# One tuned hybrid backbone: weights' low parts on VectorE, merge products queued behind the large ones, more large products in the merges

## The chip, the cores and the metric

The kernel runs on one core of one Trainium2 chip. The metric is device time in microseconds (us) of one launch; less is better. The median before is 4449.08 us over 3 runs (4446.22 to 4451.25). Engines: PE is TensorE, DVE is VectorE, ACT is ScalarE, POOL is GpSimd, SP issues DMAs.

## The reference

Two layers over 768 tokens (256 of context, 512 latent), width 1024, all in float32. Each layer projects its normalized input once and feeds three branches, of which the first is what matters here:

```
zl = hl @ w_in                       # 10112 columns: RWKV, convolution, attention, gates
def step(S, inp):                    # RWKV-7, both directions, 16 heads of 64
    r_t, w_t, k_t, v_t, kk_t, a_t = inp
    s_kk = einsum('bhij,bhj->bhi', S, kk_t)
    S = S * w_t - s_kk * (kk_t * a_t) + v_t * k_t
    return S, einsum('bhij,bhj->bhi', S, r_t)
out = sum_n(gate_n * (branch_n @ w_branch_n)) @ w_out
x   = x + mod * rms_norm(out);  x = x + mod * rms_norm(relu(h @ w1)**2 @ w2)
```

The second layer needs its output for the latent tokens only.

## The kernel before

**Large products.** Every matrix product with a weight is taken as three products of rounded parts: high times high, high of the weight times low of the operand, low of the weight times high of the operand (lines 409 to 414). `weight_half` (line 367) loads half a weight block (512 rows by 128 columns), ACT rounds it to its high part `wh` (line 328), and the remainder `wl = raw - wh` is taken by POOL when `lo_pool` is set (line 330) and else by DVE (line 332). There are three buffers each of `wh` and `wl`, and a half serves four steps of the contraction. `fill(n)` issues n such steps from a list of waiting jobs: six matmuls of 384 columns each over all 768 tokens, or three of 512 columns over the latent ones. Twenty-four matmuls use a half of the first kind, twelve one of the second.

**Recurrence.** The scan is cut in 12 chunks of 64 tokens and worked in eight rounds per layer, a pair of heads in each (`rwkv_phase`, from line 1127). A round turns on one serial path. `rw_front` makes the chunks' Gram matrices on PE (lines 809, 818) and DVE masks them (813). `rw_solve` inverts 32 by 32 triangular blocks on DVE: two transposes (854, 855), 30 pairs of a multiply (860) and an add (861) that depend on each other one by one, and two transposes back (862, 863). `rw_merge` joins the blocks for the two directions: 24 products of 32 by 32 each (891), copies by ACT (895), products again (904), copies and masks (900, 906). Then come `rw_batch` (920, 931), the chain over the chunks (`rw_chain`, 952 to 970) and, beside it, the next pair's keys and Grams, the convolution's 31 taps on DVE (470, 473) and the shift mixing of new inputs on DVE (657).

**What sets the order.** `weave` runs the parts as generators; each yields a time in us, and `pe` issues as many large products as that time by a ratio from `SCHED` calls for. While DVE solves, `fill(F['solve'] - 8)` has PE do large products (lines 1194 and 1235): 24 steps in layer 0, 32 in layer 1. The framework then schedules the recorded instructions by a cost model of its own and sets the order on each engine; an engine runs its queue in that order. Only what `keep_in_program_order` or `add_manual_dep` names is held in place: ACT's copies of line 895 stand behind the last high part of a weight. `pin` is never true, so the line that it guards does nothing.

`lo_pool` is False for the first inputs of a layer and its first solve, becomes True before the eight rounds (line 1195) and stays so through the phase that merges the branches; the MLP sets it to False.

Of the kernel before, what the change touches and what calls it, by code (L numbers as in the profile page):

```python
# [12 lines left out]
AF = mybir.ActivationFunctionType  # L13
# [6 lines left out]
KT = 8  # L20
# [24 lines left out]

SCHED = [dict(open=1.3, first=0.55, mid=0.5, end=0.4, solve=32, early=4, tap0=1, tap1=1, merge=0, sums=0, grams=0, rest=9, ln=9, pad=1, last=1.15, tap2=1),
         dict(open=1.2, first=0.4, mid=0.4, end=0.4, solve=40, early=5, tap0=0.8, tap1=0.8, merge=0, sums=0, grams=0, rest=9, ln=9, pad=1, last=0.85, tap2=1.1)]


def shape_constants():
# [24 lines left out]
class Kern:  # L77
# [319 lines left out]
    def fill(s, n=1):  # L397
        nc = s.nc
        for _ in range(min(n, len(s.jobs))):
            k, mh, ml, T, done, pre = s.jobs.pop(0)  # L400
            if k % 4 == 0:
                while s.halves and len(s.ready) < s.nw:
                    s.ready.append(s.weight_half(*s.halves.pop(0)))
                s.cur = s.ready.pop(0)
            if k == 0:
                s.jps = s.mm()
                s.jctx = (pre(),) if pre else ()
            wh, wl = s.cur
            for w, m, f in ((wh, mh, 0), (wh, ml, 1), (wl, mh, 2)):
                a = m(k)  # L410
                for b, t0, t1 in s.pieces(T):
                    ins = nc.tensor.matmul(s.jps[:, b, :t1 - t0], lhsT=w[:, k % 4, :], rhs=a[:, t0:t1], start=k == 0 and f == 0, stop=k == KT - 1 and f == 2)  # L412
                    if s.pin and f == 0 and b == 0:
                        s.tc.keep_in_program_order(ins)
            if k == KT - 1:
                done(s.jps, *s.jctx)

# [461 lines left out]
        nc.scalar.activation(out=bv[:, o:], in_=bv[:, o:], func=AF.Identity, bias=P['v']('rw_ln_b')[:, p:p + 1])  # L879
        nc.sync.dma_start(s.bv_d[p % 2][:, o:], bv[:, o:])  # L880

    def rw_merge(s, Q, d):

        nc, hi = s.nc, s.last_hi
        GL = s.big['GL', d]
        Dn, Dt = (s.Z[:, i:i + 384].rearrange("p (u t) -> p u t", t=32) for i in (1152 * d, 768 - 384 * d))
        one, two, c = (HI, LO, 0) if d else (LO, HI, 32)
        xp = s.g([128, 12, 32])
        for q in range(12):
            for h in range(2):  # L890
                nc.tensor.matmul(xp[two[h], q, :], lhsT=GL[one[h], h, q, c:c + 32], rhs=Dn[one[h], q, :], start=True, stop=True)
        TT = Q['TT', d] = GL.rearrange("p h c t -> p (h c t)")[:, 0:768].rearrange("p (c t) -> p c t", t=64)
        Xn = Dn
        for h in range(2):
            ins = nc.scalar.activation(out=Xn[two[h]], in_=xp[two[h]], func=AF.Copy, scale=-1.0)

            s.tc.add_manual_dep(ins.ins, hi.ins.name, mybir.DependencyInfo(mybir.DependencyClass.NoSync, mybir.DependencyReason.DATA), reason="weights first")
        yield 1.1 + s.sched['merge']
        for o, m in ((0, s.tlo), (32, s.thi)):
            nc.vector.tensor_scalar(out=TT[:, :, o:o + 32], in0=Dt, scalar1=m, scalar2=None, op0=ALU.mult)  # L900
        tr = s.g([128, 12, 32])
        for q in range(12):
            for h in range(2):
                nc.tensor.matmul(tr[one[h], q, :], lhsT=Xn[two[h], q, :], rhs=Dt[two[h], q, :], start=True, stop=True)
        for h in range(2):
            nc.scalar.activation(out=TT[one[h], :, c:c + 32], in_=tr[one[h]], func=AF.Copy, scale=-0.5)
        yield 1.1 + s.sched['merge']
# [171 lines left out]
    def run(s):  # L1079
        nc, tc, i = s.nc, s.tc, s.i  # L1080
        s.nraw, s.nw, s.lo_pool, s.turn = 2, 3, False, 0
        s.halves, s.ready, s.jobs = [], [], []
        s.cops, s.pin = [], False
        s.psum('gen')
        s.constants()
        s.xT_d = s.dp.tile([D, TOK], F32, name="xT_d")
        s.bv_d = [s.dp.tile([128, TOK], F32, name=f"bv_d{i}") for i in range(2)]
        s.oat = s.dp.tile([D, TOK], F32, name="oat")
        s.orw = s.dp.tile([D, TOK], F32, name="orw")
        s.ocv = s.dp.tile([D, TOK], F32, name="ocv")  # L1090
        s.spills = ([(C_Q + 128 * j, False, False) for j in range(8)] + [(C_AK + 128 * j, True, False) for j in range(4)] +
                    [(C_GATE + 128 * j, False, True) for j in range(24)])
        s.z = s.dp.tile([128 * len(s.spills), TOK], F32, name="z")
        s.kp = lambda d: d.rearrange("(k p) t -> p k t", p=128)
        PP = [s.load_params(0)]
        s.h_open()
        with ExitStack() as xc:
            X = xc.enter_context(tc.tile_pool(name="x0", bufs=1)).tile([128, KT, TOK], F32, name="X")
            sp = xc.enter_context(tc.tile_pool(name="n0", bufs=1))
            s.load_x(sp, X)  # L1100
            ss = s.ps2()
            for k in range(KT):
                s.ss_add(sp, ss, X[:, k], k, TOK)
            R = s.rstd(sp, ss, TOK, 1.0 / D, 0, CTX)
            for f in s.mod_steps(0, PP[0], sp, 0, 5):
                f()
            s.mod_pre(PP[0])
# [19 lines left out]
    def rwkv_phase(s, l, P, T):  # L1127
# [3 lines left out]
        with ExitStack() as rc:  # L1131
# [50 lines left out]
            s.rw_inputs(l, P, 0, T, I, 'krv')  # L1182
            s.fill(24)
            Q = s.rw_open(l, 0)
            s.pin = False
            spills(F['early'])
            s.weave(F['open'], prep(0, I, Q, lambda n: ()))
            s.conv_jobs(l, P, 0, T, s.ocv)
# [2 lines left out]
            s.rw_solve()  # L1191
            s.weave(3.0, rest(I))
            s.rw_inputs(l, P, 1, T, In, 'kr')
            s.fill(F['solve'] - 8)
            s.lo_pool = True
            old = None
            for p in range(8):
                ev = set()
# [14 lines left out]
                else:  # L1213
                    spills(len(todo))
                s.tratio = F['tap0'] if more else 1.2
                held = [s.rw_readout(l, P, p - 1, old, T, s.orw), note('ro')] if old else [note('ro')]
                gs = [chain(s.rw_merge(Q, 0), s.rw_batch(Q, 0, lat), note('b0'), wait('b1'), s.rw_chain(Q, lat, ev.add, wait('ro'))),
                      chain(s.rw_merge(Q, 1), s.rw_batch(Q, 1, lat), note('b1'))]
                if more:
                    gs.append(chain(prep(p + 1, In, Qn, wait, *held), wait('s3'), grams(In, Qn, 0), wait('s7'), grams(In, Qn, 1), wait('s11'), grams(In, Qn, 2)))  # L1220
                else:
# [4 lines left out]
                if more:  # L1226
# [5 lines left out]
                    s.weave(3.0, rest(I))  # L1232
                    if p < 6:
                        s.rw_inputs(l, P, p + 2, T, In, 'kr')
                    s.fill(F['solve'] - 8)
            s.taps(len(s.cops))
            s.pin = False

    def merge_phase(s, l, PP, T, acc):

# [208 lines left out]
```

## Time and profile before

| | |
|---|---|
| median of 3 runs | 4449.08 us |
| profiled execution, its own time | 4455.6 us |
| its span, first to last instruction | 4453.8 us |
| busy share of the span: PE, PEld, DVE, ACT, POOL | 94%, 77%, 60%, 41%, 19% |
| mean granted clock of TensorE | 0.956 of 2.4 GHz |
| recurrence of layer 0, of layer 1 | 150 to 1240 us, 2550 to 3580 us |

The span is 1.8 us shorter than the execution's own time. Windows are stretches of the span: for each engine busy us and, in brackets, the instructions begun, in the order PE, PEld, DVE, ACT, POOL; PEclk is the share of TensorE's full clock that was granted, as a mean over the stretch. The granted clock has two levels, 1.2 and 2.4 GHz.

### The profile page before, as it was taken

How to read it: one execution, taken by the hardware profiler on the slowest of the kernel's cores; microseconds unless marked ns; L12 is line 12 of the kernel's file. 1: busy time of each engine (PE TensorE's matmuls, PEld its weight loads, DVE VectorE, ACT ScalarE, POOL GpSimd, SP SyncE). 2: the span in 40 equal slices, each digit the busy share in tenths (PEclk: the TensorE clock that was granted, in tenths of full speed). 3: DMA queues.
4: the chain of work that ended last, by engine and by line, in shares of the span. 5: the costliest groups of instructions: out<-in, count | busy, mean ns of one | idle time of the engine just before them, and what ended most of it. 6: DMA issues, size and time to landing. Idle time of an engine off the chain costs nothing. (4 is left out here: it accounts for less than half of the span.)

```text
span 4453.8 us, 76934 instructions
## 1 busy us (share of the span) xinstructions
PE 4190.7 (94%) x31232; PEld 3412.5 (77%) x31232; DVE 2674.6 (60%) x4828; ACT 1817.7 (41%) x3562; POOL 837.4 (19%) x735
## 2 busy tenths in 40 slices
PE   6999999999998989899999899999999988898998
PEld 4888887888886678689999677877777775475886
DVE  3788778878945453232233568778778854443344
ACT  3454445444434442332222344545444534434332
POOL 0022121212112145300000102122122212262001
PEclk8999999999999999899999889999999979998999
DMA  4211211111134235343322221121111233142332
GB/s 166 66 46 52 60 59 55 57 50 57 60 96 163 68 97 166 119 149 129 103 79 64 66 60 56 48 61 49 54 54 59 65 104 101 57 140 63 96 95 81
DMA packets 438345, 364.05 MB, mean 82 GB/s; under 512 B 19022, under 2 KB 386792, under 8 KB 431848
## 3 DMA queue, kind: packets, MB, share of 16 engines
q1 hardware_dynamic: 417256, 279.43, 20.8%
q10 hardware_dynamic: 20736, 79.70, 4.9%
q8 instruction: 247, 4.05, 0.4%
q14 instruction: 106, 0.87, 0.1%
HBM read 299.29 MB, written 53.48 MB: 79 GB/s over the span
## 5 line engine op out<-in xcount | busy, mean ns | idle before, releaser
L328 ACT ACTIVATE wh<-raw 128x512 fp32r<-128x512 f32 x700 | 441.9, 631 | 1332.1 <-PE mm L389 561.2
L330 POOL TENSOR_TENSOR wl<-raw,wh 128x512 fp32r<-128x512 f32 x386 | 534.2, 1384 | 2008.5 <-ACT wh L328 1697.7
L412 PE MATMUL mm<-hh,wh 128*128 128x384 f32 (+1 forms) x2072 | 668.1, 381 | 11.6 <-ACT hh L347 4.0
L412 PE MATMUL mm<-hl,wh 128*128 128x384 f32 (+1 forms) x2072 | 647.9, 371 | 7.0 <-POOL hl L330 7.0
L412 PE MATMUL mm<-hh,wl 128*128 128x384 f32 (+1 forms) x2072 | 641.9, 369 | 0.0
L332 DVE TENSOR_TENSOR wl<-raw,wh 128x512 fp32r<-128x512 f32 x314 | 216.6, 691 | 579.3 <-ACT wh L328 575.7
L473 DVE SCALAR_TENSOR_TENSOR cv<-u,dw,cv 128x783 f32<-128x783 f32 (+1 forms) x480 | 453.6, 945 | 2.9
L412 PEld LDWEIGHTS mm<-hh,wh 128*128 128x128 f32 x2072 | 381.1, 195 | 70.5 <-issue 19.0
L412 PEld LDWEIGHTS mm<-hl,wh 128*128 128x128 f32 x2072 | 390.2, 195 | 46.2 <-issue 10.5
L412 PEld LDWEIGHTS mm<-hh,wl 128*128 128x128 f32 x2072 | 391.1, 195 | 38.5 <-issue 12.1
L412 PE MATMUL mm<-oh,wh 128*128 128x384 f32 (+1 forms) x768 | 252.4, 383 | 11.2 <-DVE acc L1275 5.8
L412 PE MATMUL mm<-ol,wh 128*128 128x384 f32 (+1 forms) x768 | 240.0, 365 | 11.6 <-POOL ol L330 11.6
L389 PE MATMUL mm<-hh,wh 128*128 128x384 f32 (+1 forms) x768 | 238.5, 365 | 6.3 <-ACT hh L347 3.6
L412 PE MATMUL mm<-oh,wl 128*128 128x384 f32 (+1 forms) x768 | 240.0, 365 | 2.3 <-POOL wl L330 2.2
L389 PE MATMUL mm<-hl,wh 128*128 128x384 f32 (+1 forms) x768 | 236.7, 362 | 5.8 <-POOL hl L330 5.3
L389 PE MATMUL mm<-hh,wl 128*128 128x384 f32 (+1 forms) x768 | 234.8, 361 | 0.0
L389 PE MATMUL mm<-fh,wh 128*128 128x384 f32 (+1 forms) x768 | 230.2, 353 | 0.0
L389 PE MATMUL mm<-fh,wl 128*128 128x384 f32 (+1 forms) x768 | 230.0, 353 | 0.0
L389 PE MATMUL mm<-fl,wh 128*128 128x384 f32 (+1 forms) x768 | 229.8, 353 | 0.0
L860 DVE TENSOR_TENSOR Z<-A 128x30 f32<-128x30 f32 (+14 forms) x480 | 202.5, 422 | 16.6
L861 DVE TENSOR_TENSOR A<-A,Z 128x30 f32<-128x30 f32 (+14 forms) x480 | 201.8, 420 | 15.9
L412 PEld LDWEIGHTS mm<-oh,wh 128*128 128x128 f32 x768 | 140.1, 190 | 56.0 <-ACT wh L328 12.8
(294 smaller groups left out, 7404.4 us busy)
## 6 DMA issues: line engine op xcount, KB each, us to landing
raw<-in_w_in_dram SPq DMA_DIRECT2D x316, 256.0 KB
raw<-in_w_ff_dram SPq DMA_DIRECT2D x256, 256.0 KB
wmod<-in_w_mod_dram ACTq DMA_DIRECT2D x48, 1024.0 KB
raw<-in_w_branch_dram SPq DMA_DIRECT2D x96, 256.0 KB
z<-f ACTq DMA_DIRECT2D x40, 384.0 KB
gt<-z SPq DMA_DIRECT2D x24, 384.0 KB
raw<-in_w_out_dram SPq DMA_DIRECT2D x32, 256.0 KB
z<-f ACTq DMA_DIRECT2D x32, 256.0 KB
```

Of the source, the lines that this page charges most:

```text
L328: s.last_hi = nc.scalar.activation(out=hi, in_=src, func=AF.Copy)
L330: nc.gpsimd.tensor_tensor(out=lo, in0=src, in1=hi.bitcast(F32), op=ALU.subtract)
L332: nc.vector.tensor_tensor(out=lo, in0=src, in1=hi.bitcast(F32), op=ALU.subtract)
L389: nc.tensor.matmul(ps[:, b, :t1 - t0], lhsT=w[:, k % 4, :], rhs=a[:, t0:t1], start=k == 0 and f == 0, stop=k == KT - 1 and f == 2)
L412: ins = nc.tensor.matmul(s.jps[:, b, :t1 - t0], lhsT=w[:, k % 4, :], rhs=a[:, t0:t1], start=k == 0 and f == 0, stop=k == KT - 1 and f == 2)
L473: s.tap_pin(nc.vector.scalar_tensor_tensor(out=hold['c'], in0=u[:, k:k + L], scalar=w(k), in1=hold['c'], op0=ALU.mult, op1=ALU.add))
L860: nc.vector.tensor_tensor(out=tm, in0=X[:, k + 1:, k:k + 1].to_broadcast([128, n, k]), in1=X[:, k:k + 1, 0:k].to_broadcast([128, n, k]), o ...
L861: nc.vector.tensor_tensor(out=X[:, k + 1:, 0:k], in0=X[:, k + 1:, 0:k], in1=tm, op=ALU.add)
```

## The change

1. `lo_pool` is no longer set in the recurrence, so `wl` is taken by DVE there, and in the phase that merges the branches too, which set nothing itself.
2. The first products of both merges (line 891 before, 893 after) get a queue-order dependence on `mm`, the last large product issued before the round. ACT's copies of both merges stand behind the same high part `hi`, read before the round begins.
3. `fill(F['solve'] - 8)` becomes `fill(F['solve'])` with 26 and 34 in place of 32 and 40: 26 steps in place of 24, and 34 in place of 32. `merge` goes from 0 to 1.2 and 1.4, so that each of the two stages of a merge yields 2.3 or 2.5 us in place of 1.1.
4. `pin` is taken out.

```diff
-SCHED = [dict(... solve=32, ... merge=0, ...), dict(... solve=40, ... merge=0, ...)]
+SCHED = [dict(... solve=26, ... merge=1.2, ...), dict(... solve=34, ... merge=1.4, ...)]
...
-                    ins = nc.tensor.matmul(s.jps[:, b, :t1 - t0], ...)
-                    if s.pin and f == 0 and b == 0:
-                        s.tc.keep_in_program_order(ins)
+                    s.last_mm = nc.tensor.matmul(s.jps[:, b, :t1 - t0], ...)
...
+    def behind(s, ins, other):
+        s.tc.add_manual_dep(ins.ins, other.ins.name, mybir.DependencyInfo(mybir.DependencyClass.NoSync, mybir.DependencyReason.DATA), reason="queue order")
...
-    def rw_merge(s, Q, d):
-        nc, hi = s.nc, s.last_hi
+    def rw_merge(s, Q, d, hi, mm):
+        nc = s.nc
...
-                nc.tensor.matmul(xp[two[h], q, :], lhsT=GL[one[h], h, q, c:c + 32], rhs=Dn[one[h], q, :], start=True, stop=True)
+                s.behind(nc.tensor.matmul(xp[two[h], q, :], lhsT=GL[one[h], h, q, c:c + 32], rhs=Dn[one[h], q, :], start=True, stop=True), mm)
...
-            ins = nc.scalar.activation(out=Xn[two[h]], in_=xp[two[h]], func=AF.Copy, scale=-1.0)
-            s.tc.add_manual_dep(ins.ins, hi.ins.name, ..., reason="weights first")
+            s.behind(nc.scalar.activation(out=Xn[two[h]], in_=xp[two[h]], func=AF.Copy, scale=-1.0), hi)
...
-            s.fill(F['solve'] - 8)
-            s.lo_pool = True
+            s.fill(F['solve'])
...
+                mm = s.last_mm
-                gs = [chain(s.rw_merge(Q, 0), ...), chain(s.rw_merge(Q, 1), ...)]
+                gs = [chain(s.rw_merge(Q, 0, s.last_hi, mm), ...), chain(s.rw_merge(Q, 1, s.last_hi, mm), ...)]
```

How it moves instructions is shown at one solve of layer 1, the sixth, and the merge after it. On PE, before, the large products of the solve end here (`mm` is their sum, `hh`, `hl` the operand's parts, `wh`, `wl` the weight's), and both directions' first merge products follow (`Z` holds the inverted blocks):

```order
L412 MATMUL mm<-hh,wh 128x512
L412 MATMUL mm<-hl,wh 128x512
L412 MATMUL mm<-hh,wl 128x512
L891 MATMUL g<-Z,GL_22404 32x32 x24
L891 MATMUL g<-Z,GL_22409 32x32 x24
L412 MATMUL mm<-hh,wh 128x384 x2
L412 MATMUL mm<-hl,wh 128x384 x2
L412 MATMUL mm<-hh,wl 128x384 x2
L412 MATMUL mm<-hh,wh 128x384 x2
```

On PE now, the same place:

```order
L412 MATMUL mm<-hl,wh 128x512
L412 MATMUL mm<-hh,wl 128x512
L412 MATMUL mm<-hh,wh 128x512
L893 MATMUL g<-Z,GL_22404 32x32 x24
L412 MATMUL mm<-hl,wh 128x512
L412 MATMUL mm<-hh,wl 128x512
L412 MATMUL mm<-hh,wh 128x512
L893 MATMUL g<-Z,GL_22409 32x32 x24
L714 MATMUL g<-cst,ksq 128x2 x6
L412 MATMUL mm<-hl,wh 128x512
L412 MATMUL mm<-hh,wl 128x512
```

The two directions' products stand apart, with three large products between them. Between the last Gram product of the round and the first merge product stand 164 large products where there were 110. In the other solves of layer 1 the counts go from 120, 128, 208, 115, 128 to 132, 143, 197, 136, 159 before this one, and from 125 and 99 to 163 and 120 behind it. In layer 0 they go from 171, 202, 212, 209, 192, 175, 209, 132 to 183, 220, 193, 149, 156, 155, 176, 189.

On DVE, before, the solve's last pairs and the transposes back, with the shift mixing of `in_k` begun at the very end:

```order
L860 TENSOR_TENSOR Z<-A 128x58
L861 TENSOR_TENSOR A<-A,Z 128x2x29
L860 TENSOR_TENSOR Z<-A 128x30
L657 SCALAR_TENSOR_TENSOR in_k<-f_30088,H,in_k 128x255
L861 TENSOR_TENSOR A<-A,Z 128x30
L657 SCALAR_TENSOR_TENSOR in_k<-f_30088,H,in_k 128x511
L862 STREAM_TRANSPOSE Z<-A 128x32x32
L657 SCALAR_TENSOR_TENSOR in_k<-f_30088,H,in_k 128x255
L863 STREAM_TRANSPOSE Z<-A 128x32x32
L657 SCALAR_TENSOR_TENSOR in_k<-f_30088,H,in_k 128x511
L900 TENSOR_SCALAR GL_22404<-Z,cst 128x12x32 x2
L900 TENSOR_SCALAR GL_22409<-Z,cst 128x12x32
```

On DVE now, a stretch of the same solve some eight pairs ahead of its end (lines 860 and 861 have become 858 and 859, 473 has become 471):

```order
L471 SCALAR_TENSOR_TENSOR cv<-u,dw,cv 128x512
L858 TENSOR_TENSOR Z<-A 128x168
L471 SCALAR_TENSOR_TENSOR cv<-u,dw,cv 128x512
L859 TENSOR_TENSOR A<-A,Z 128x7x24
L471 SCALAR_TENSOR_TENSOR cv<-u,dw,cv 128x512
L858 TENSOR_TENSOR Z<-A 128x150
L471 SCALAR_TENSOR_TENSOR cv<-u,dw,cv 128x512
L859 TENSOR_TENSOR A<-A,Z 128x6x25
L332 TENSOR_TENSOR wl<-raw,wh 128x512
L858 TENSOR_TENSOR Z<-A 128x130
L332 TENSOR_TENSOR wl<-raw,wh 128x512
L859 TENSOR_TENSOR A<-A,Z 128x5x26
```

Pairs that stood one behind the other now have convolution taps and low parts of weights between them. Inside this solve stand 9 low parts, 5 instructions of the convolution's taps, 10 of shift mixing and 1 that makes the convolution's input; before it had 1 of that kind, 2 of shift mixing, and no low part. The solves of the other rounds hold 4 to 9 low parts; the fourth to sixth of layer 0 and the fourth to seventh of layer 1 hold 5 to 15 taps and shifts besides, and the eighth of layer 0 ten taps.

On POOL no low part of a weight is left (386 before). On DVE there are 386 more.

## Rows read from the trace of the kernel before

**Rows 1.** Page, part 5: low parts on GpSimd (count; busy us, mean ns; idle before, releaser)

```profile
L330 POOL TENSOR_TENSOR wl<-raw,wh 128x512 fp32r<-128x512 f32 x386 | 534.2, 1384 | 2008.5 <-ACT wh L328 1697.7
```

**Rows 2.** Windows, both recurrences (columns: busy us of each engine, PEclk, DMA share, GB/s)

```profile
150.00:1240.00 1090.00, 1066.48 (x10638) 906.22 (x10638) 912.32 (x1665) 499.70 (x1069) 212.69 (x206) 0.98 0.19 57
2550.00:3580.00 1030.00, 980.43 (x9370) 767.19 (x9368) 828.10 (x1593) 498.42 (x1074) 200.17 (x209) 0.93 0.19 57
```

**Rows 3.** Waits of TensorE, second recurrence (us in total, times, longest)

```profile
PE g L891 <- DVE Z L862: 29.3, 7, 7.6
```

**Rows 4.** Windows of 26 us at the eight merges of layer 1

```profile
2640.00:2666.00 26.00, 24.43 (x297) 21.48 (x296) 16.14 (x35) 10.08 (x21) 1.37 (x2) 0.80 0.17 48
2770.00:2796.00 26.00, 22.20 (x273) 18.85 (x273) 18.24 (x43) 10.39 (x19) 3.82 (x3) 0.67 0.11 31
2910.00:2936.00 26.00, 25.97 (x357) 22.61 (x356) 14.50 (x34) 14.31 (x28) 5.96 (x5) 1.00 0.19 53
3037.00:3063.00 26.00, 19.72 (x253) 17.10 (x253) 20.36 (x44) 8.88 (x16) 3.38 (x3) 0.67 0.11 32
3165.00:3191.00 26.00, 20.26 (x249) 17.68 (x248) 19.17 (x43) 8.93 (x16) 3.89 (x3) 0.67 0.11 32
3300.00:3326.00 26.00, 17.93 (x260) 17.10 (x260) 18.31 (x45) 7.84 (x14) 2.61 (x2) 0.67 0.11 32
3430.00:3456.00 26.00, 21.18 (x274) 17.74 (x273) 18.84 (x42) 10.80 (x20) 3.82 (x3) 0.67 0.08 22
3563.00:3589.00 26.00, 18.44 (x285) 14.48 (x283) 18.74 (x32) 12.07 (x30) 2.32 (x2) 0.67 0.23 70
```

**Rows 5.** Windows of 26 us at merges of layer 0

```profile
214.00:240.00 26.00, 24.05 (x298) 23.36 (x298) 18.70 (x36) 8.25 (x15) 2.59 (x2) 0.87 0.15 42
796.00:822.00 26.00, 26.00 (x346) 24.28 (x344) 21.19 (x36) 14.80 (x28) 6.75 (x5) 1.00 0.15 42
935.00:961.00 26.00, 23.69 (x278) 22.08 (x277) 18.93 (x37) 10.37 (x17) 4.81 (x4) 0.74 0.11 32
1226.00:1252.00 26.00, 20.10 (x285) 18.40 (x283) 23.82 (x34) 9.57 (x21) 2.56 (x2) 0.67 0.31 97
```

**Rows 6.** Windows of two solves, line 860 alone (VectorE busy, count)

```profile
2617.50:2648.40 30.90, 9.89 (x30) 1.00 0.32 90
3273.20:3307.80 34.60, 12.94 (x30) 0.93 0.25 71
```

**Rows 7.** The same windows, line 861 alone

```profile
2617.50:2648.40 30.90, 9.95 (x30) 1.00 0.32 90
3273.20:3307.80 34.60, 14.15 (x30) 0.93 0.25 71
```

**Rows 8.** The second window, line 330 alone (GpSimd busy, count)

```profile
3273.20:3307.80 34.60, 9.36 (x7) 0.93 0.25 71
```

**Rows 9.** Timeline of VectorE, first solve (start us, us long)

```profile
205.78 0.40 DVE L861 TENSOR_TENSOR A<-A,Z 128x228 f32<-128x228 f32 x1
206.21 0.39 DVE L860 TENSOR_TENSOR Z<-A 128x220 f32<-128x220 f32 x1
206.52 0.68 DVE L332 TENSOR_TENSOR wl<-raw,wh 128x512 fp32r<-128x512 f32 x1
207.12 0.38 DVE L861 TENSOR_TENSOR A<-A,Z 128x220 f32<-128x220 f32 x1
```

**Rows 10.** Timeline of TensorE, two large products of the sixth solve of layer 1

```profile
3285.86 0.39 PE L412 MATMUL mm<-hl,wh 128*128 128x512 f32 x1
3286.09 0.40 PE L412 MATMUL mm<-hh,wl 128*128 128x512 f32 x1
```

**Rows 11.** Who waited for line 332, 150 to 330 us (us, times)

```profile
  PEld mm L412: 0.3, 1
```

**Rows 12.** Waits of TensorE, 1600 to 1660 us

```profile
PE g L504 <- POOL csum L501: 8.4, 1, 8.4
```

**Rows 13.** Timeline of GpSimd there

```profile
1618.27 2.01 POOL L330 TENSOR_TENSOR wl<-raw,wh 128x512 fp32r<-128x512 f32 x1
```

More of the change, by code (lines that the diff above doesn't have):

```diff
@@ L44 @@
 VOFF = {n: 8 * i for i, n in enumerate(VECS)}
-SCHED = [dict(open=1.3, first=0.55, mid=0.5, end=0.4, solve=32, early=4, tap0=1, tap1=1, merge=0, sums=0, grams=0, rest=9, ln=9, pad=1, last=1.15, tap2=1),
-         dict(open=1.2, first=0.4, mid=0.4, end=0.4, solve=40, early=5, tap0=0.8, tap1=0.8, merge=0, sums=0, grams=0, rest=9, ln=9, pad=1, last=0.85, tap2=1.1)]
+SCHED = [dict(open=1.3, first=0.55, mid=0.5, end=0.4, solve=26, early=4, tap0=1, tap1=1, merge=1.2, sums=0, grams=0, rest=9, ln=9, pad=1, last=1.15, tap2=1),
+         dict(open=1.2, first=0.4, mid=0.4, end=0.4, solve=34, early=5, tap0=0.8, tap1=0.8, merge=1.4, sums=0, grams=0, rest=9, ln=9, pad=1, last=0.85, tap2=1.1)]
 def shape_constants():
@@ L411, in fill @@
                 for b, t0, t1 in s.pieces(T):
-                    ins = nc.tensor.matmul(s.jps[:, b, :t1 - t0], lhsT=w[:, k % 4, :], rhs=a[:, t0:t1], start=k == 0 and f == 0, stop=k == KT - 1 and f == 2)
-                    if s.pin and f == 0 and b == 0:
-                        s.tc.keep_in_program_order(ins)
+                    s.last_mm = nc.tensor.matmul(s.jps[:, b, :t1 - t0], lhsT=w[:, k % 4, :], rhs=a[:, t0:t1], start=k == 0 and f == 0, stop=k == KT - 1 and f == 2)
             if k == KT - 1:
@@ L894, in rw_merge @@
         for h in range(2):
-            ins = nc.scalar.activation(out=Xn[two[h]], in_=xp[two[h]], func=AF.Copy, scale=-1.0)
-            s.tc.add_manual_dep(ins.ins, hi.ins.name, mybir.DependencyInfo(mybir.DependencyClass.NoSync, mybir.DependencyReason.DATA), reason="weights first")
+            s.behind(nc.scalar.activation(out=Xn[two[h]], in_=xp[two[h]], func=AF.Copy, scale=-1.0), hi)
         yield 1.1 + s.sched['merge']
@@ L1082, in run @@
         s.halves, s.ready, s.jobs = [], [], []
-        s.cops, s.pin = [], False
+        s.cops = []
         s.psum('gen')
@@ L1184, in rwkv_phase @@
             Q = s.rw_open(l, 0)
-            s.pin = False
             spills(F['early'])
@@ L1215, in rwkv_phase @@
                 s.tratio = F['tap0'] if more else 1.2
+                mm = s.last_mm
                 held = [s.rw_readout(l, P, p - 1, old, T, s.orw), note('ro')] if old else [note('ro')]
-                gs = [chain(s.rw_merge(Q, 0), s.rw_batch(Q, 0, lat), note('b0'), wait('b1'), s.rw_chain(Q, lat, ev.add, wait('ro'))),
-                      chain(s.rw_merge(Q, 1), s.rw_batch(Q, 1, lat), note('b1'))]
+                gs = [chain(s.rw_merge(Q, 0, s.last_hi, mm), s.rw_batch(Q, 0, lat), note('b0'), wait('b1'), s.rw_chain(Q, lat, ev.add, wait('ro'))),
+                      chain(s.rw_merge(Q, 1, s.last_hi, mm), s.rw_batch(Q, 1, lat), note('b1'))]
                 if more:
@@ L1234, in rwkv_phase @@
                         s.rw_inputs(l, P, p + 2, T, In, 'kr')
-                    s.fill(F['solve'] - 8)
+                    s.fill(F['solve'])
             s.taps(len(s.cops))
-            s.pin = False
     def merge_phase(s, l, PP, T, acc):
```

## The prediction

> **What bounds the kernel now.** I read the page first: TensorE is busy 94% of the span, so what can be won is TensorE's idle time and the time that it spends at the lower clock. The windows by stage come next [rows 2]: the recurrence of layer 0 has 1066 busy us in 1090 at a granted clock of 0.98, that of layer 1 only 980 in 1030 at 0.93. The waits of TensorE in layer 1 then name the place [rows 3]: 29.3 us, in seven waits of up to 7.6, stand before the first merge product and end with VectorE's transpose that closes the solve. Large products are queued behind that waiting product on TensorE, as the order of before shows, and can't pass it.
>
> What a wait costs is more than its idle time. For each merge I take a window of 26 us and count it as lost where TensorE is idle or at the lower clock: 26 less busy time times granted clock [rows 4, 5]. In layer 1 this gives 6.5, 11.1, 0, 12.8, 12.4, 14.0, 11.8 and 13.7, together 82 us; the 0 is the one merge that TensorE reached late, with other work still to do when the solve was over. In layer 0 the first merge loses 5.1, the sixth 8.5, the eighth 12.5; the fifth stands for the five that TensorE reached late, of which the other four lie between 0 and about 3.5 (I take 1.5 each). Together 32 us. So 114 us of the profiled 4455.6 are lost around the sixteen merges.
>
> **What a low part costs on either engine.** GpSimd takes 1.38 us for one [rows 1], VectorE 0.68 [rows 9]. But VectorE pays for GpSimd's as well. The thirty multiplies and thirty adds of a solve take 9.9 + 10.0 = 19.8 us in the first round of layer 1, where the low parts are already VectorE's, and 12.9 + 14.2 = 27.1 in the sixth, where GpSimd does seven [rows 6 to 8]. That is 7.3 us, or 1.04 for each low part. On VectorE a low part between two dependent steps of the solve costs less than its duration: the multiply and add around one begin 0.91 us apart, the pair before it 0.43 [rows 9], so 0.48. I take 0.5 for any insert of 512 columns in a solve, 0.3 for one of 256; elsewhere 0.60, from the start of the low part to that of the next instruction in the same rows.
>
> The Trainium skill's page "Perfetto Trace Analysis", in Optimizing Scalar/DVE Operations, says that work may be taken off a saturated VectorE and given to another engine, GpSimd even; read by itself, this speaks against the change, since VectorE is busy 80 to 84% of the recurrences [rows 2]. It adds that the two share a read port, so that the move might not help. The solve rows agree with the second half; that VectorE becomes the bound all the same is the last rival below.
>
> **The change part by part.**
>
> *Low parts.* In the recurrences 235 low parts move (116 in layer 0, 119 in layer 1, by the order and the stages). At 0.60 they bring VectorE 141 us. In the fourteen solves that have GpSimd's (five in each of layer 0, six to eight in layer 1, 87 in all) it gets back 87 x 1.04 = 90. What it gets back outside the solves no row separates: between 0 and 1.04 for each of the other 148, so the bill lies between +51 and -103 us on 1740 busy. I take about zero, in the middle, since convolution taps fill VectorE there and a part of the low parts must meet them. Whether VectorE's queue delivers in time is the other question: around the first solve of layer 0, where it makes them, TensorE waited for one of them 0.3 us, once [rows 11].
>
> *The sixth solve of layer 1, worked out.* Before, it takes 34.6 us. It loses seven GpSimd low parts, -7.3. It gets 9 low parts (4.5), 6 long and 4 short shift instructions in place of one each (2.5 + 0.9), and 5 taps (2.5): +10.4. The solve ends 3.1 us later. TensorE in turn gets 54 more large products ahead of the merge; one of 512 columns follows the next after 0.23 us at full clock [rows 10], one of 384 after three quarters of that; the order's mix gives 9.7 us. TensorE idles 8.1 us in this merge's window [rows 4]: 8.1 + 3.1 - 9.7 leaves 1.5 us.
>
> *The other merges, the same way.* In layer 1 the first to third and the eighth come out covered. The fourth, fifth and seventh keep 2 to 3.5 us of wait, because their solves hold shifts and taps as well. In layer 0 the fourth to sixth have 60, 36 and 20 products of 384 columns fewer ahead of the merge (0.175 us each, so 10, 6 and 3.5 us): the first two use up their lead, the sixth, which waited already, keeps some 3 us. The eighth gains 57 products, 9.9 us against 5.9 of idle time. So I count five merges with a short wait and eleven without.
>
> *What these cost.* Short waits are dear, since the clock falls all the same: the second merge of layer 1 idled 3.8 us and lost 11.1, the sixth of layer 0 idled 2.3 and lost 8.5 [rows 4, 5]. I take 9 for each of the five, 45 us. For the eleven I take 1.3, the mean of the late ones of layer 0: 14 us. Left are 59 of the 114: -55.
>
> *More products between the merge's stages.* 1.2 to 1.4 us more in each of four yields, times the ratio of 0.4 to 0.55, makes some 2.5 steps a round. With the two steps more in `fill` they are taken from later in the same round. TensorE's work is the same; but chain and Grams have less to fill their gaps with. I take 0.5 us a round as lost, +8, with bounds 0 (chain and Grams hide each other) and 40 (all that is moved, 2.5 us in each of sixteen rounds, leaves a gap).
>
> *Merging of the branches.* GpSimd has 128 + 23 low parts fewer there. At one place TensorE waits for its sum of squares, 8.4 us [rows 12], with two low parts in GpSimd's queue among the sums, one of 2.01 us [rows 13] and one about as long as the mean of rows 1: -3.4, and about as long a stall of the clock shortened; with the same place in layer 1 I take -5, bounds 0 and -15. The attention's and the LayerNorm's work on VectorE gets 0.6 us later per low part, with VectorE busy less than half of the time; I cost this at nothing, covered by the large products of the other branch, and at up to +10 where that cover is short.
>
> *Nothing.* `pin` is never set. The common `hi` lets ACT's second copies stand no later than before.
>
> **The sum.** 4455.6 - 55 - 5 + 8 = 4403.6 for the profiled execution. It was 6.5 us slower than the median of the runs shown, so I forecast 4397.
>
> **The rivals.**
>
> *All merges are covered.* The solve's inserts fall into gaps that dependent steps leave anyway, and TensorE reaches every merge late, as it does the third of layer 1 with no loss. Then 16 x 1.3 = 21 remain of the 114: 4449 - 93 - 5 = 4351. Against it stand the counts above, in which two engines run level for five solves.
>
> *The gain is eaten.* Low parts now wait behind a solve step, and solve steps behind shifts that need the large products which need those low parts: two queues that hold each other up for 3 to 4 us in each of the fourteen solves give back the 55. Then it is 4449, give or take 9. For it: little idle time is enough, as the sixth merge of layer 0 shows. Against it: the first solves of both layers run in this way now and lose 5.1 and 6.5, the least of the merges with any wait.
>
> *VectorE becomes the bound, and the kernel slower.* If the stalls come back only in the solves (+51 us on VectorE) and VectorE's waits for the Grams can't be squeezed, TensorE waits for low parts. The place is the stretch of keys and taps ahead of the Grams, where VectorE has no idle time. It decides from 0.22 us of wait per half: 235 x 0.22 = 52 eats the gain. At 0.4 it is 4397 + 94 = 4491. Against it speaks the one wait of 0.3 us [rows 11], but that stretch has no readout and few taps.
>
> **How the numbers follow.** Forecast 0.50, its own range 4372 to 4428 (four merges more or fewer with a wait, at 8 each, and the bounds of the smaller terms). All covered 0.20, eaten 0.17, slower 0.13. The whole range goes from 4345, under the second case, to 4452, just over the third; it leaves out the fourth. A change below 0.2% (8.9 us) can't be told from none. Faster: 0.49 + 0.20 + 0.04 = 0.73; the same: 0.01 + 0.12 + 0.01 = 0.14; slower: 0.01 + 0.12 = 0.13.
>
> **What would show it.** In the profile after, the recurrence of layer 1 should have a granted clock of 0.96 or more and be shorter by about 40 us, that of layer 0 by about 10. The multiplies and adds of each solve should sum to 20 us, as in rows 6 and 7. TensorE's waits before the first merge product should fall from 29.3 us to about 10, in five or so waits. The prediction is wrong if TensorE waits for low parts on VectorE for more than 30 us, if the waits before the merge are still above 25, or if new idle time appears in chain and Grams.

## The result and the profile after

The changed kernel takes 4398.59 us (median of 4 runs, 4393.04 to 4402.83) against 4450.16 for the kernel before in the same session. The ratio is 0.988, 95% interval 0.986 to 0.9901. So it is faster by 1.2%, and the forecast of 4397 came within 2 us. Two of the steps that led there were wrong by 22 and 24 us, with opposite signs, so that the sum came out this close is luck; the experiments below show it.

The page: VectorE took the 386 low parts and its busy time rose by only 33 us, from 2674.6 to 2707.6, though at 0.72 us each (mean of the last row) they make 277. GpSimd's row of low parts [rows 1] has no counterpart any more.

```profile
PE 4190.7 (94%) x31232; PEld 3412.5 (77%) x31232; DVE 2674.6 (60%) x4828; ACT 1817.7 (41%) x3562; POOL 837.4 (19%) x735
```

```profile
PE 4180.3 (95%) x31232; PEld 3410.6 (77%) x31232; DVE 2707.6 (62%) x5214; ACT 1819.4 (41%) x3562; POOL 289.9 (7%) x349
L332 DVE TENSOR_TENSOR wl<-raw,wh 128x512 fp32r<-128x512 f32 x700 | 501.6, 718 | 710.7 <-ACT wh L328 699.1
```

The stages come next. I cut them at the first product of the keys, the last output product of the chain and the first product of the MLP, so that each window holds the same part of the program. First the kernel before: recurrence and merging of the branches of layer 0, then of layer 1 (columns as in [rows 2]).

```profile
131.10:1340.10 1209.00, 1185.46 (x11783) 1010.18 (x11782) 965.26 (x1767) 548.89 (x1170) 228.79 (x218) 0.98 0.19 60
1340.10:1880.20 540.10, 494.21 (x2466) 383.68 (x2464) 227.56 (x402) 209.53 (x376) 180.40 (x119) 0.97 0.39 126
2553.80:3645.20 1091.40, 1041.83 (x9976) 817.09 (x9974) 855.26 (x1660) 520.52 (x1131) 206.54 (x214) 0.92 0.19 57
3645.20:4061.60 416.40, 357.88 (x1382) 236.08 (x1380) 180.55 (x313) 168.91 (x314) 155.49 (x117) 0.95 0.32 100
```

The same four stages of the changed kernel:

```profile
131.10:1334.90 1203.80, 1189.21 (x11813) 1015.19 (x11814) 950.85 (x1896) 551.14 (x1172) 28.05 (x90) 0.99 0.20 61
1334.90:1863.80 528.90, 486.63 (x2436) 378.16 (x2435) 263.48 (x468) 209.04 (x375) 94.97 (x53) 0.97 0.39 127
2535.50:3599.70 1064.20, 1042.46 (x10023) 822.15 (x10023) 836.09 (x1788) 523.86 (x1137) 31.07 (x90) 0.93 0.20 60
3599.70:4006.70 407.00, 350.03 (x1334) 230.30 (x1334) 211.11 (x378) 165.55 (x308) 69.64 (x49) 0.93 0.31 98
```

The recurrences are 5 and 27 us shorter, the merging of the branches 11 and 9. The counts of TensorE's instructions show that the recurrences also took over work: 30 large products more in layer 0 and 47 in layer 1, and as many fewer in the stages behind them (30 and 48). VectorE's busy time fell from 965 to 951 and from 855 to 836 us with the low parts on board.

The waits before the first merge product [rows 3] went from 29.3 us in seven to 5.4 in five; in layer 0, the second row, there are four:

```profile
PE g L893 <- DVE Z L860: 5.4, 5, 1.3
```

```profile
PE g L893 <- DVE Z L860: 4.8, 4, 1.4
```

The windows of 26 us at the merges of layer 1, each begun some 8 us ahead of the merge as in [rows 4]; the second and third, left out here, have 25.94 and 26.00 busy us at full clock:

```profile
2624.00:2650.00 26.00, 25.93 (x323) 23.38 (x323) 23.01 (x53) 11.87 (x20) 0.00 (x0) 1.00 0.22 63
...
3005.00:3031.00 26.00, 24.79 (x286) 21.59 (x285) 21.61 (x50) 9.99 (x18) 0.00 (x0) 0.87 0.12 34
3138.00:3164.00 26.00, 24.92 (x331) 20.02 (x329) 23.11 (x52) 13.51 (x27) 0.00 (x0) 1.00 0.28 85
3266.00:3292.00 26.00, 25.02 (x302) 19.92 (x302) 18.74 (x44) 9.63 (x19) 0.00 (x0) 0.87 0.31 93
3395.00:3421.00 26.00, 24.68 (x263) 19.63 (x263) 17.70 (x44) 8.72 (x16) 0.00 (x0) 0.74 0.27 82
3524.50:3550.50 26.00, 24.53 (x342) 19.03 (x342) 21.89 (x40) 15.48 (x37) 0.00 (x0) 0.87 0.32 95
```

Counted in the prediction's way (26 less busy time times clock), they lose 0.1, 0.1, 0, 4.4, 1.1, 4.2, 7.7 and 4.7, together 22 us where it was 82. In layer 0 five windows lose something; the first, sixth and eighth, as [rows 5]:

```profile
216.00:242.00 26.00, 23.51 (x279) 21.61 (x278) 16.30 (x28) 8.18 (x14) 0.00 (x0) 0.77 0.14 42
...
941.00:967.00 26.00, 24.73 (x281) 23.08 (x280) 22.09 (x40) 8.90 (x16) 0.00 (x0) 0.74 0.11 32
1238.00:1264.00 26.00, 23.88 (x371) 20.39 (x371) 23.72 (x39) 17.03 (x41) 0.00 (x0) 1.00 0.50 159
```

These lose 7.9, 7.7 and 2.1, the fourth and fifth 1.5 and 4.7: 24 us against 32. So the merges gave back 68 of 114 us.

The sixth solve of layer 1, line 858 alone and then line 859 alone, as [rows 6, 7]:

```profile
3235.10:3273.60 38.50, 9.81 (x30) 1.00 0.27 75
```

```profile
3235.10:3273.60 38.50, 9.88 (x30) 1.00 0.27 75
```

The lengthening is gone: 19.7 us in the sixth solve, where it was 27.1.

### The profile page after: what moved, and what is told of

Read it like the earlier page. It is cut to its first block, busy times and chain, and to the rows that moved or that the text cites. A ratio compares the mean times of both kernels' runs of the same rounds, so it can differ in the third digit from the quotient of the medians.

```text
span 4401.0 us, 76934 instructions
## 1 busy us (share of the span) xinstructions
PE 4180.3 (95%) x31232; PEld 3410.6 (77%) x31232; DVE 2707.6 (62%) x5214; ACT 1819.4 (41%) x3562; POOL 289.9 (7%) x349
## 4 chain that ended last, share of the span: by engine, by line
PE 81%; DVE 8%; ACT 4%; issue 2%; POOL 2%; DMA 2%; SPq 0%; ACTq 0%; POOLq 0%; DVEq 0%
PE mm L412 32%; PE mm L389 20%; PE g L807 4%; PE g L633 2%; PE g L931 2%; PE g L920 2%; PE sp L952 2%; PE g L1032 2%; PE sp L956 1%; PE S L612 1%; PE yp L970 1%; PE g L842 1%; PE yp L968 1%; PE g L816 1%; PE g L234 1%
## 5 line engine op out<-in xcount | busy, mean ns | idle before, releaser
L332 DVE TENSOR_TENSOR wl<-raw,wh 128x512 fp32r<-128x512 f32 x700 | 501.6, 718 | 710.7 <-ACT wh L328 699.1
L412 PE MATMUL mm<-hh,wh 128*128 128x384 f32 (+1 forms) x2072 | 654.2, 373 | 10.2 <-ACT hh L347 4.0
L471 DVE SCALAR_TENSOR_TENSOR cv<-u,dw,cv 128x783 f32<-128x783 f32 (+1 forms) x480 | 425.7, 887 | 2.7
L389 PE MATMUL mm<-hh,wh 128*128 128x384 f32 (+1 forms) x768 | 239.1, 366 | 6.4 <-ACT hh L347 3.6
L807 PEld LDWEIGHTS g<-KR,BK 64*128 64x128 f32 x1536 | 156.6, 206 | 36.8 <-issue 32.4
L807 PE MATMUL g<-KR,BK 64*128 64x128 f32 (+1 forms) x1536 | 176.4, 307 | 1.8 <-DVE KR L800 1.6
L958 ACT ACTIVATE S<-sp,lam 128x64 f32<-128x64 f32 x352 | 92.1, 310 | 191.6 <-PE sp L956 182.0
```

The costliest lines, as they stand in the source:

```text
L332: nc.vector.tensor_tensor(out=lo, in0=src, in1=hi.bitcast(F32), op=ALU.subtract)
L389: nc.tensor.matmul(ps[:, b, :t1 - t0], lhsT=w[:, k % 4, :], rhs=a[:, t0:t1], start=k == 0 and f == 0, stop=k == KT - 1 and f == 2)
L412: s.last_mm = nc.tensor.matmul(s.jps[:, b, :t1 - t0], lhsT=w[:, k % 4, :], rhs=a[:, t0:t1], start=k == 0 and f == 0, stop=k == KT - 1 and ...
L471: s.tap_pin(nc.vector.scalar_tensor_tensor(out=hold['c'], in0=u[:, k:k + L], scalar=w(k), in1=hold['c'], op0=ALU.mult, op1=ALU.add))
L807: nc.tensor.matmul(gp[h][:, q, 0:n, :], lhsT=BK[ROWS[h], 4 * g + q].rearrange("p a b -> p (a b)"), rhs=KR[ROWS[h], 0:n, 4 * g + q, :], sta ...
L958: nc.scalar.activation(out=Sn[:, d], in_=sp[:, d], func=AF.Copy, scale=Q['lam', d][:, q[d]:q[d] + 1])
```

## The experiments

Undoing the parts alone and together gives most of the answer. In the table "low" stands for low parts on VectorE, R in the recurrence and B in the merging of the branches; steps are those beside each solve; merge is the number in SCHED. Ratios are to the kernel before in the same session; the medians of before in the three sessions of the experiments were 4455.8 (e1 to e4), 4447.1 (e5 to e8) and 4451.3 (e9 to e12).

| kernel | low | steps | merge | us | ratio, 95% interval |
|---|---|---|---|---|---|
| changed kernel | R, B | 26, 34 | 1.2, 1.4 | 4398.6 | 0.988 (0.986 to 0.9901) |
| e1 | R, B | 24, 32 | 0 | 4366.1 | 0.9809 (0.9793 to 0.9825) |
| e2 | none | 26, 34 | 1.2, 1.4 | 4470.0 | 1.0043 (1.0029 to 1.0058) |
| e3 | R, B | 26, 34 | 0 | 4387.0 | 0.9844 (0.9828 to 0.986) |
| e4 | R | 26, 34 | 1.2, 1.4 | 4414.1 | 0.9906 (0.9883 to 0.9928) |
| e5 | B | 24, 32 | 0 | 4420.2 | 0.9942 (0.9926 to 0.9958) |
| e6 | solves of R, B | 24, 32 | 0 | 4397.7 | 0.9892 (0.9872 to 0.9911) |
| e7 | R but its solves, B | 24, 32 | 0 | 4418.2 | 0.9933 (0.9917 to 0.995) |
| e8 | R, B | 22, 30 | 0 | 4393.6 | 0.9883 (0.986 to 0.9906) |
| e9 | as changed, no dependence | 26, 34 | 1.2, 1.4 | 4396.6 | 0.9861 (0.9831 to 0.9891) |
| e10 | R, B | 24, 32 | 1.2, 1.4 | 4382.0 | 0.9835 (0.9807 to 0.9864) |
| e11 | R, B | 25, 33 | 0 | 4368.7 | 0.9813 (0.9787 to 0.984) |
| e12 | R, B | 23, 31 | 0 | 4388.2 | 0.9842 (0.9815 to 0.987) |

### The parts one by one

**e1, low parts alone.** The diff against the kernel before:

```diff
-            s.lo_pool = True
             old = None
```

> The kernel before with one part of the change: low parts on VectorE in the recurrence and in the merging of the branches; SCHED, the number of steps and the dependences as before. Theory A (the low parts are the lever: without GpSimd's work beside it each solve gets shorter, and VectorE's queue then has large products set ahead of the merges): most of the gain is here, 4400 to 4420 us; TensorE's waits before the first merge product of layer 1 fall from 29.3 us to under 15. Theory B (the numbers in SCHED are the lever, the low parts only make room for them): under 15 us of the gain is here, 4435 us or more.

Measured 4366, 90 us below before (85 by the ratio) and 32 below the changed kernel, with intervals apart. This is below theory A's range, a larger gain than it asked for; only e11 comes as low. The waits before the first merge product of layer 1 are 4.5 us, with the steps beside each solve as before:

```profile
PE g L893 <- DVE Z L860: 4.5, 4, 1.9
```

But the scheduler made another order once the low parts were VectorE's. Counted in the trace as the counts ahead of the prediction are, e1 has 135, 136, 124, 134, 127 and 121 large products ahead of the second and the fourth to eighth merge of layer 1, where before had 128, 115, 128, 110, 125 and 99. So these merges get shorter solves and 72 more large products at once, without a step added in SCHED.

Its four stages, cut as above:

```profile
133.50:1312.70 1179.20, 1168.39 (x11783) 995.38 (x11783) 954.45 (x1895) 549.50 (x1170) 45.68 (x90) 0.99 0.20 61
1312.70:1839.10 526.40, 490.89 (x2464) 383.15 (x2464) 260.81 (x469) 210.65 (x376) 95.08 (x53) 0.97 0.40 129
2510.40:3570.50 1060.10, 1029.33 (x9975) 806.02 (x9975) 838.14 (x1784) 520.25 (x1131) 35.47 (x90) 0.94 0.20 59
3570.50:3971.10 400.60, 351.67 (x1380) 233.30 (x1380) 213.17 (x382) 168.87 (x314) 69.12 (x49) 0.97 0.33 104
```

Each stage gained: 30 and 31 us in the recurrences, 14 and 16 in the merging of the branches. Where they come from is seen in the groups of VectorE's instructions (count; busy us, mean ns; idle before), first of the kernel before:

```profile
L473 DVE SCALAR_TENSOR_TENSOR cv<-u,dw,cv 128x783 f32<-128x783 f32 (+1 forms) x480 | 453.6, 945 | 2.9
L860 DVE TENSOR_TENSOR Z<-A 128x30 f32<-128x30 f32 (+14 forms) x480 | 202.5, 422 | 16.6
L861 DVE TENSOR_TENSOR A<-A,Z 128x30 f32<-128x30 f32 (+14 forms) x480 | 201.8, 420 | 15.9
L813 DVE TENSOR_TENSOR GL<-g,masks 128x256 f32<-128x256 f32 x192 | 80.3, 420 | 120.8 <-PE g L809 120.4
```

Then of e1:

```profile
L471 DVE SCALAR_TENSOR_TENSOR cv<-u,dw,cv 128x783 f32<-128x783 f32 (+1 forms) x480 | 425.2, 886 | 2.1
L858 DVE TENSOR_TENSOR Z<-A 128x30 f32<-128x30 f32 (+14 forms) x480 | 158.1, 329 | 14.8
L859 DVE TENSOR_TENSOR A<-A,Z 128x30 f32<-128x30 f32 (+14 forms) x480 | 158.8, 331 | 14.1
L811 DVE TENSOR_TENSOR GL<-g,masks 128x256 f32<-128x256 f32 x192 | 80.2, 419 | 91.4 <-PE g L807 90.9
```

The multiplies and adds of the solves fell by 44 + 43 = 87 us, the taps by 28. The masks of the Grams kept their 420 ns. This is the pattern that the Trainium skill's page "SBUF — State Buffer" gives in Who interferes with whom: a VectorE instruction with two inputs in SBUF contends with a GpSimd instruction that reads SBUF, one with at most one such input doesn't, outside its two-port modes. The masks read the Grams from PSUM (`g`) and have one input in SBUF; the trace agrees with both halves. The trace of before alone shows it as well: 63 of the 480 multiplies overlap a low part of GpSimd for at least half of their time and take 1043 ns on average, the 398 that overlap none take 326; for the adds it is 1034 and 328. The masks of line 813 take 416 ns beside a low part and 418 without.

**e2, SCHED alone.**

```diff
-... solve=32, ... merge=0, ...), dict(... solve=40, ... merge=0, ...)
+... solve=26, ... merge=1.2, ...), dict(... solve=34, ... merge=1.4, ...)
-            s.fill(F['solve'] - 8)
+            s.fill(F['solve'])
```

> The kernel before with the numbers in SCHED and two more steps per solve alone; low parts stay on GpSimd, no dependences. Theory A: the solves keep their 7 us of lengthening, the large products ahead of the fourth to eighth merge of layer 1 are as many as before (111, 109, 109, 125, 108 against 115, 128, 110, 125, 99), so the waits stay; 4440 to 4465 us, no gain or a small loss. Theory B: 4410 us or less.

Measured 4470, ratio 1.0043: slower, by about 19 us, 5 us above theory A's range. What theory A said of the order is so: 111, 109, 109, 125 and 108 large products stand ahead of the fourth to eighth merge of layer 1, no more in all than before. So e2 has the numbers of SCHED, but not more products where TensorE waits. The waits at the merges of layer 1 are even longer than the 29.3 of before:

```profile
PE g L893 <- DVE Z L860: 32.7, 6, 9.5
```

**e3, the changed kernel with merge at 0.**

```diff
-merge=1.2 ... merge=1.4
+merge=0 ... merge=0
```

> The changed kernel with merge set back to 0 in both layers, all else as changed. Theory A (more products between the stages of a merge shift later work into the next solve, which puts 10 to 30 large products more ahead of the fourth to seventh merge of layer 1): without it these merges wait 2 to 5 us longer each and the time is 4408 to 4425 us. Rival (the products taken from chain and Grams cost there what they bring at the merges): the same as the changed kernel, within 8 us of 4399.

Measured 4387, so neither: the merge numbers do not help, they cost some 12 us, with intervals that just touch. **e10** has them without the longer solves, on e1:

> Low parts on VectorE and merge at 1.2 and 1.4; the steps per solve as before (24 and 32). Theory A (the merge numbers take products from the head of the attention, where the changed kernel waits 5.8 us for kT and 9.7 for vz and the kernel with merge at 0 only 1.6 and 1.2): those two waits are over 4 us each, and the time is 4373 to 4385 us, 7 to 19 above the low parts alone. Rival (the merge numbers cost only together with the longer solves): 4360 to 4370 us.

Measured 4382, in theory A's range, 16 above e1; the two intervals overlap, so the time alone would not settle it. The place named does, though in layer 1 the wait is for `kT` and not for `vz`. These are TensorE's waits at the head of the attention (line 521), layer 0 and then layer 1, of e3, of the changed kernel, and of e10:

```profile
PE g L521 <- DVE kT L581: 1.6, 1, 1.6
PE g L521 <- DMA vz<-z: 1.2, 1, 1.2
```

```profile
PE g L521 <- DVE kT L581: 5.8, 1, 5.8
PE g L521 <- DMA vz<-z: 9.7, 1, 9.7
```

```profile
PE g L521 <- DVE kT L581: 5.7, 1, 5.7
PE g L521 <- DVE kT L581: 7.8, 1, 7.8
```

That is 15.5 and 13.5 us with the merge numbers, 2.8 without. The recurrences draw 30 and 48 large products forward in the changed kernel, 30 and 40 in e10 and none in e3, so these products were what covered the waits. The other place is the chain over the chunks. TensorE's busy time in one of its four lines, 952, in the recurrence of layer 0, first of the changed kernel, then of e1:

```profile
131.10:1334.90 1203.80, 46.70 (x704) 31.57 (x704) 0.99 0.20 61
```

```profile
133.50:1312.70 1179.20, 40.97 (x704) 28.37 (x704) 0.99 0.20 61
```

The same instructions cover 6 us more; with lines 956, 968 and 970 it is 15, and 8 in layer 1. (Records overlap; counted only up to the start of the next matmul, the four lines take 11 and 8 us more.) In layer 1 the stretches from the first to the last product of the eight chains, counted in the trace, hold 231 large products in the changed kernel, 301 in e1, and are as long in all (340 and 341 us). This is the loss of filling that the prediction feared, but not as idle time: TensorE idles there 4.4 us against 3.7. It spends 31.8 us there at the lower clock against 20.5, which alone could be some 6 of the 8 us. In layer 0 the stretches hold more, 668 against 590, and a chain takes 45 to 56 us in place of 35 to 45 in the first seven rounds, with 4.3 us idle against 2.0. e10 has the same (658, 45 to 55 us), so it comes from the merge numbers; what lengthens the chains there stays open.

**e9, no dependence.**

```diff
-                s.behind(nc.tensor.matmul(xp[two[h], q, :], ...), mm)
+                nc.tensor.matmul(xp[two[h], q, :], ...)
-        nc = s.nc
+        nc, hi = s.nc, s.last_hi
```

> The changed kernel without the dependence of the merge products on the last large product, and ACT's copies behind the high part that each merge finds for itself, as before the change. The scheduler's order on every engine is the same row for row, so by theory A the time is that of the changed kernel, 4390 to 4405 us. Rival (the dependence acts where the order doesn't show it): outside 4385 to 4412 us.

Measured 4396.6. Row for row, every engine has the order of the changed kernel in the trace, so this part of the change does nothing, and the gap of 2 us between the two shows how far one program's medians differ from session to session.

### Where the low parts matter

**e4 and e5, the merging of the branches.** e4 is the changed kernel with `s.lo_pool = True` at the end of the recurrence, e5 the kernel before with `s.lo_pool = False` there.

> The changed kernel with the low parts of the phase that merges the branches back on GpSimd (151 of them), those of the recurrence on VectorE. The forecast's term of 5 us: 4404 us, with TensorE's wait of some 8 us for the sum of squares back. Rival (the phases became 11 and 9 us shorter for this reason alone): 4415 to 4420 us. Second rival (the phases got shorter because the recurrences took products from them): 4399 us, no difference.

> The kernel before with the low parts of the merging of the branches alone on VectorE; in the recurrence on GpSimd, SCHED as before. Theory A (what the low parts alone brought is additive by stage: there the two phases became 13.7 and 15.7 us shorter): 4456 - 29 = 4427 us. Rival (the forecast's term of 5 us, the rest came from the recurrence's end): 4445 to 4452 us.

e4 took 4414, 15 above the changed kernel, with a wide spread (4395 to 4423): nearest to the rival's range, but its interval overlaps that of the changed kernel. e5 is clear: 4420, 27 below before, 7 below theory A's number, and the forecast's 5 us is refuted. The stages of e5 came out 16 and 17 us shorter than before. The wait that the prediction had singled out, 8.4 us for the sum of squares [rows 12], is only one piece:

```profile
PE g L502 <- POOL csum L499: 5.3, 1, 5.3
```

The rest is spread over the attention's steps on VectorE, which GpSimd had lengthened as it did the solve. Lines 623 and 617 of before, from 1340 to 1629 us, and TensorE's wait for the first:

```profile
L623 DVE TENSOR_SCALAR Pm<-Pm,st 128x768 f32<-128x768 f32 (+1 forms) x48 | 31.7, 659 | 0.9
L617 DVE TENSOR_REDUCE st<-S 128x1 f32<-128x768 f32 (+1 forms) x48 | 37.0, 770 | 25.1 <-PE S L614 23.0 <-PE S L610 2.1
```

```profile
PE g L630 <- DVE Pm L623: 4.5, 9, 1.7
```

The same of e5 (lines 621 and 615):

```profile
L621 DVE TENSOR_SCALAR Pm<-Pm,st 128x768 f32<-128x768 f32 (+1 forms) x48 | 28.7, 598 | 0.9
L615 DVE TENSOR_REDUCE st<-S 128x1 f32<-128x768 f32 (+1 forms) x48 | 36.9, 770 | 21.4 <-PE S L612 21.4
```

```profile
PE g L628 <- DVE Pm L621: 1.8, 1, 1.8
```

The Trainium skill's page "SBUF — State Buffer", in Who interferes with whom, counts tensor_scalar among the instructions that can take the shared ports in a two-port mode, where their operands allow it, and says that tensor_reduce never does on trn2; the trace agrees. The reduction kept its 770 ns, though it reads `S` from PSUM, so that this row can't tell that rule from the one on a single SBUF input. The scaling of `Pm` got 61 ns shorter, 48 times, and the wait for it fell from 4.5 to 1.8 us. Most of the attention's other waits shrank too, by up to 2.4 us.

**e6 and e7, in the solves or outside them.** Both have the branches' low parts on VectorE, as e5. In e6 `lo_pool` is False from the start of each `rw_solve` to the end of its `fill`, else True; in e7 the reverse.

> As the run before it, with the low parts that are issued from the start of a solve to the end of its large products on VectorE too; GpSimd keeps those that come in the rest of each round. Theory A (the stalls in the solves are what matters, 87 of them at 1.04 us): most of the recurrences' 61 us, 4375 to 4395 us, TensorE's waits before the first merge product of layer 1 under 15 us. Rival (VectorE gets back as much outside the solves): 4395 to 4415 us.

> The reverse: low parts issued in a solve on GpSimd, all others on VectorE. Theory A: the waits before the merge stay above 20 us in layer 1 and the time is 4410 to 4430 us. Rival: 4380 to 4400 us.

By the ratios, the solves alone bring 22 us on top of e5, the others alone 4 (the intervals of e7 and e5 overlap), both together 59 (e1). e6 came out 3 us past theory A's range, in the rival's, with waits of 15.5 us where under 15 were expected. e7 has theory A's time, but waits of 7.4 where over 20 were expected: its taps, on a VectorE that GpSimd leaves alone outside the solves, take 888 ns (945 before), and TensorE's row has more large products ahead of the later merges (135, 123, 115, 134, 112 against 115, 128, 110, 125, 99 from the fourth on). And where a low part is issued is not where it runs: e6's last solve of layer 1 still holds seven GpSimd low parts and waits 7.2 us for its merge. Waits at the merges of layer 1, of e6 and then of e7:

```profile
PE g L893 <- DVE Z L860: 15.5, 6, 7.2
```

```profile
PE g L893 <- DVE Z L860: 7.4, 5, 3.1
```

Ahead of those five merges e6 has 122, 120, 123, 127 and 101 large products. So each placing of the low parts also gives another order, and no run changes the stalls under one order: how much of a half's time is the stall and how much the order is not separated. The solves weigh most; why the two halves together bring twice their sum stays open.

### How many products beside a solve

e8, e11 and e12 are e1 with two steps fewer, one more and one fewer for each solve.

> Low parts on VectorE everywhere and, in SCHED, two steps fewer for each solve than before the change (22 and 30, merge at 0). Theory A (with the shorter solves 24 and 32 are level; fewer leave TensorE 1.4 to 2.1 us short at each merge, and the clock falls there): 4378 to 4395 us, 12 to 25 above the low parts alone (4366). Rival (each step beside the solve is one that chain and Grams lack, so two fewer gain what two more cost): 4345 to 4360 us.

> Low parts on VectorE, one step more for each solve (25 and 33), merge at 0. Theory A (the count of steps has a flat best value at 24 and 32, two more cost 21 us, two fewer 28): between the two, 4368 to 4384 us. Rival (each count gives the scheduler another order, whose gaps and clock falls differ by chance): a time that doesn't lie between, under 4364 or over 4388 us.

> The same with one step fewer for each solve (23 and 31). Theory A: 4370 to 4390 us. Rival: under 4364 or over 4394 us.

In order of steps (22, 23, 24, 25, 26 in layer 0; 30 to 34 in layer 1) the medians are 4394, 4388, 4366, 4369 and 4387; by the ratios they stand 33, 15, 0, 2 and 16 us above e1, and the interval of one step fewer overlaps e1's. All three times lie in theory A's ranges: the old count, or one more, is the best of the five. But the reason that theory A gave is not what the traces show. The scheduler sets nearly as many large products ahead of the fourth to eighth merge of layer 1 whatever the count (637, 637, 642, 641 and 647 together), and in the one profiled execution of each, the merges of e8 and e12 lose less than e1's (43 and 27 us against 49, in windows that begin 8 us ahead of each merge), not more. What grows with fewer steps is another wait of TensorE in the recurrence of layer 1, for `key`, first of e8, then of e1:

```profile
PE g L874 <- DVE key L868: 16.1, 7, 4.2
```

```profile
PE g L874 <- DVE key L868: 7.8, 4, 3.7
```

In e12 it is 12.8 us, in e11 9.7. So the rival, that each count gives another order with gaps of its own, is not excluded. Why two more cost as much as they do is not settled. In the profile of e3 the recurrence of layer 1 is 15 us longer than in e1 without more idle time; TensorE spent 171 us of it at the lower clock, 130 in e1, and one execution each doesn't say whether that is the rule.

## Why the prediction was right, step by step

- **The price of a GpSimd low part in a solve, 1.04 us: right.** It gave 90 us for 87 low parts; the two lines fell by 87 in e1.
- **The sixth solve, worked out: right.** Its chain was to end 3.1 us later and leave TensorE idle for 1.5; it takes 38.5 us in place of 34.6, 3.9 later, and leaves 1.0 (26 less 25.02 busy).
- **The merges, -55: right in kind, 13 us short.** They gave 68. Nine merges wait where five were expected, but each loses 4.2 us on average, not the 9 that was taken from the second of layer 1 and the sixth of layer 0.
- **What covers the merges: right in kind, wrong in where the products come from.** The working laid it to shorter solves and to more large products ahead of them, and took the products from the order of the whole change. e1 has both as well: its six waits in layer 1 fell by some 25 us, and 72 more products at 0.23 us [rows 10] are at most 16.6 of it. Of the 54 extra products of the sixth solve, 24 come with the low parts alone (134 in e1); the merge numbers bring the other 30 or so (163 in e10), ahead of a solve that taps and shifts then lengthen; longer solves in SCHED bring none (134 in e3). At the merges these numbers buy little: counted in the prediction's way, all sixteen lose 49 us in e1 and 46 in the changed kernel. What more products would do without shorter solves is not shown, since e2 hasn't got them.
- **VectorE outside the solves, "about zero, in the middle": a slip.** The middle of the bounds +51 and -103 is -26. VectorE's busy time in the recurrences of e1 fell from 1821 to 1793 us, by 28.
- **"I cost this at nothing, covered", in the merging of the branches: the step that failed first.** The term was -5 with bounds of 0 and -15, though its own working gave 3.4 of idle time and as much of the clock at one place of layer 0 alone; low parts alone bring 27 (e5). I looked at one wait for GpSimd and at the delay that a low part adds to VectorE's queue, not at the lengthening of the attention's own instructions, though I had measured that for the solve.
- **"Chain and Grams have less to fill", +8: the step that failed second.** SCHED costs 32 on top of the low parts (changed kernel against e1), within the bounds of 0 and 40 but far from the value taken. Hardly any of it is the idle time in chains and Grams that the term was for: that is 3 us more in the chains of both layers and less before the Grams. Another 13 are waits at the attention's head, a place that the prediction did not name. TensorE's time in the lines of the chains is 23 longer; 8 of them, in layer 1, go with fewer products there and more time at the lower clock, 15, in layer 0, stay open. In the four stages together the profile of the changed kernel has 263 us at the lower clock, that of e1 197. These counts overlap and come from one execution each, so they can't be added up to the 32.
- **The sum.** By the ratios, the low parts bring 85 and SCHED costs 32, which leaves 53. The forecast's 52 is that number because the two errors above nearly cancel: that is luck.
- **The rivals.** VectorE did not become the bound: TensorE's weight loads waited once for a low part on it, 0.3 us, in the whole changed kernel's recurrences. This speaks against the two queues of "eaten" too; SCHED did eat 32 us, but elsewhere. "All covered", 4351, is nearest to e1 in its number, but not in its mechanism: e1's merges still lose 49 us where that rival left 21.
- **The tests.** Each solve's multiplies and adds were to sum to 20 us: all sixteen take 19.6 to 19.9. Waits of about 10 us in five: 5.4 in five, and 4.8 in four of layer 0, where I had expected one. Layer 1 was to be 40 us shorter at a clock of 0.96; it is 27 shorter at 0.93, with 47 more products in it (0.23 us each, 11 us). Layer 0: 10 forecast, 5 measured, with 30 more (5 us). None of the signs of being wrong came up: 0.3 us of waits for low parts, 5.4 before the merges, no new idle time worth the name in chain and Grams.

## What to carry to other kernels

Before work is put on GpSimd to relieve VectorE, compare the same VectorE instruction with and without GpSimd beside it, in every stage where both run: the stall that is paid in a chain of dependent steps, here 1 us for each 1.4 us low part, costs more than the instruction saves. A change of several parts should be timed part by part: here one part brings 90 us, one loses 32 and one does nothing, and the whole does not show it. Compare the order on each engine as well: a scheduler that is given the same numbers made another order once the low parts had moved, and set nearly the same number of products ahead of the later merges when the steps beside each solve were changed. Large products that cover one wait are taken from another; count what is left at the place that they leave.

## What the hardware showed that I had not expected

The clock can fall after very short pauses, and without one. In the recurrence of layer 1 of the changed kernel, from the first merge on, it falls to 1.2 GHz nine times, for 7 to 34 us each. Six of the falls come within 8 us behind a pause of 0.8 to 1.3 us: the window of the seventh merge above has 1.3 us of idle time in 26 and a granted clock of 0.74. Not each such pause has a fall behind it: the window of the fifth merge has 1.1 us of idle time at full clock. The other three follow no pause over 0.41 us in the 30 us before them, as this one, 70 us behind the sixth merge, before which TensorE is busy for 27.28 of 27.30 us:

```profile
3316.00:3343.30 27.30, 27.28 (x301) 20.01 (x301) 24.78 (x36) 18.13 (x42) 3.24 (x10) 1.00 0.10 35
3343.30:3353.50 10.20, 10.20 (x46) 8.20 (x47) 4.58 (x10) 3.48 (x7) 0.00 (x0) 0.50 0.27 78
```

Such stretches are what is left in e1: of the 130 us at the lower clock in its recurrence of layer 1, 51 stand at the merges and 79 elsewhere.
